# Gated linear attention on one core: decay levels grown in place on VectorE, the two head pairs' levels interleaved, the two heads' state products side by side

## Chip, cores and metric

The kernel runs on one core of a Trainium2 chip. The metric is the device time of one execution in microseconds (us); before the change it is 1471.57 us, the median of three runs (1470.83 to 1471.6). Engines are named as the profile names them: PE is TensorE's matmul, PEld its weight load, DVE is VectorE, ACT ScalarE, POOL GpSimd, SP SyncE.

## What is computed

One layer of a hybrid encoder on 512 tokens: an input projection, three token mixers side by side (windowed attention, short convolution, bidirectional gated linear attention, GLA), a merge, a LayerNorm, and an expert-choice mixture of 16 experts. The change touches GLA alone:

```python
def gla_direction(q, k, v, log_a):      # 4 heads, key dim 64, value dim 128
    b = jnp.cumsum(log_a..., axis=2)    # in chunks of C tokens
    diff = b[:, :, :, None] - b[:, :, None, :]
    decay = jnp.exp(jnp.where(lower, diff, -jnp.inf))
    scores = jnp.einsum('bnthd,bnshd,bntshd->bnhts', qc, kc, decay)
    o_intra = jnp.einsum('bnhts,bnshv->bnthv', scores, vc)
    ...
    o_inter = jnp.einsum('bnthd,bnhdv->bnthv', qc * jnp.exp(b), states)
    return (o_intra + o_inter).reshape(B, S, H, dv)
...
o = o_f + o_b                           # forward and backward scans, summed
```

A score between tokens t and s is the sum over the key dimension of q, k and the product of all decays between them. Without it the sum would be a plain product; with it the kernel has to scale q and k by decays before they meet.

## The kernel before

**Stages.** The trace has these: a first projection (to about 43 us), the main input projection with GLA and attention woven into it (to about 264 us), the merge (to about 480 us), output projection and routing (to about 530 us), and the experts, whose weights stream in through 10 tiles of 2 MB (to the end).

**The woven stage.** The main projection has 25 blocks of 128 output columns (`names`, from `gq0` to `cb3`). A block is 24 matmuls of 128x512 into one PSUM tile `pa` (L267 to L269). The work of GLA and of attention is a list of 43 steps. From the fifth block on the blocks are cut into segments (`SEGS`: eight blocks of three segments of 9, 9 and 6 matmuls, then blocks of two and of one), and one step stands behind each segment. Program order for step s is: its successor's `prep` (VectorE, GpSimd), the low half of a weight split (`wb`, VectorE, L256), the segment's matmuls, the step's own matmuls (`pe`), its evacuation (`post`). All engines work through their queues in that order.

**Levels.** The four heads come in two pairs (`Gla(0)`, `Gla(1)`; two heads of 64 lines fill 128 partitions). Scores are built level by level, for m = 1, 2, 4, ... 128: within each block of 2m tokens the tokens of one half meet those of the other, so that q carries the decay from the block's middle to it, and k the decay from it to the middle. `levels` lists 0 (the diagonal), these eight, 256 (transposed keys) and 257 (the state): 11 steps for each pair. Four decay arrays of 512 tokens are kept for a pair: `Pf` and `Sb` (used by q), `Sf` and `Pb` (used by k). At each level from m = 2, `prep` doubles the reach of all four, VectorE `Sf` and `Pf` (L376, L377), GpSimd `Pb` and `Sb` (L378, L379), and then forms decayed q (L385, L386, VectorE) and decayed k (L388, L389, GpSimd) anew into one of two tiles `qk2`; each of these eight takes half of the 512 tokens. Then 16 products of 64x64 (L421, for m below 128) go to `pg0` and `pg1`, and `post` puts them under a mask into `gD` (L446), or for m of 64 and 128 copies them into `A` (L442 to L452, ScalarE).

**Output.** `av_pe` (L463, L466) multiplies A by the values for each head and each of four token blocks tb, two products of 128x128 and then one with the state, whose weights and state fill 64 partitions only. `av_squares`, `av_var`, `av_norm`, `tr_pe` and `tr_post` follow in steps of their own.

**Order of the steps.** The 11 levels of pair 0, its `av_pe`; the 11 levels of pair 1, beside which the rest of pair 0's output runs; pair 1's `av_pe`; then attention (19 steps), beside whose first steps the rest of pair 1's output runs. [...]

Of the kernel before, what the change touches and what calls it, by code (L numbers as in the profile page):

```python
# [28 lines left out]
def tile_hybrid_layer(ctx, tc, pk, w2p, xT, x, wlv, wa, wak, wmb, wout, eg, eu, ed, out):  # L29
# [62 lines left out]
    Q = [128, 4, 512]  # L92
# [41 lines left out]
    gD = at_t[:, 384:896].rearrange("p (h b t) -> p h b t", h=2, b=4)  # L134
# [145 lines left out]
    adec = {}  # L280
# [53 lines left out]
        A.copy(h, src)  # L334
        later.append(lambda: V.tensor_sub(l, src, f32(h)))

    def qk_tiles():
        st["qk2"], st["gps1"] = D("qk2", [128, 2, 2, 512], [128, 2, 512])

    class Gla:  # L340


        def __init__(self, i):
            self.i = i
            self.q = gqk[:, 0, i, :]
            self.k = gqk[:, 1, i, :]
            self.w = {}
            self.levels = [0, 1, 2, 4, 8, 16, 32, 64, 128, 256, 257]

        def start(self):  # L350
            i = self.i
            if i == 0:
                self.ps, st["gA0"] = D("gps0", Q, Q)
                self.Pf, self.Sb, self.Sf, self.Pb = (self.ps[:, j, :] for j in range(4))
                adec[0, 0], adec[1, 0] = self.Pf, self.Sb
                adec[0, 1], adec[1, 1] = misc[:, 2, :], misc[:, 3, :]
            else:
                self.ps = st["gps1"]
                self.Pf, self.Sb = misc[:, 2, :], misc[:, 3, :]
                self.Sf, self.Pb = (self.ps[:, j, :] for j in range(2))  # L360
            G.memset(self.Sf, 1.0)
            G.memset(self.Pb, 1.0)

        def prep(self, m):

            if m == 0 and self.i == 1:
                self.start()
            if m == 0 or m == 257:
                return
            if m > 1:  # L370
                h = m // 2
                v = [a.rearrange("p (n two h) -> p n two h", two=2, h=h) for a in (self.Pf, self.Sb, self.Sf, self.Pb)]
                Pf, Sb, Sf, Pb = v
                n = 512 // m
                sh = [128, n, h]
# [4 lines left out]
            if "qk2" not in st:  # L380
                qk_tiles()
            w = st["qk2"][:, self.levels.index(m) % 2]
            self.w[m] = w
            r = lambda ap: ap.rearrange("p (n two h) -> p n two h", two=2, h=m)
            V.tensor_mul(r(w[:, 0, :])[:, :, 0, :], r(self.q)[:, :, 0, :], r(self.Sb)[:, :, 0, :])  # L385
            V.tensor_mul(r(w[:, 0, :])[:, :, 1, :], r(self.q)[:, :, 1, :], r(self.Pf)[:, :, 1, :])  # L386
            if m > 1:
                G.tensor_mul(r(w[:, 1, :])[:, :, 0, :], r(self.k)[:, :, 0, :], r(self.Sf)[:, :, 0, :])  # L388
                G.tensor_mul(r(w[:, 1, :])[:, :, 1, :], r(self.k)[:, :, 1, :], r(self.Pb)[:, :, 1, :])  # L389

        def pe(self, m):
            if m == 257:
                self.p = P("pst")
                for b in range(4):
                    for h in range(2):
                        head = 2 * self.i + h
                        PE.matmul(self.p[h * 64:h * 64 + 64, b // 2 * 128:b // 2 * 128 + 128],
                                  self.kt[:, b * 128 + h * 64:b * 128 + h * 64 + 64],
                                  v_sb[:, b, head * 128:(head + 1) * 128], start=b % 2 == 0, stop=b % 2 == 1)
                return  # L400
            w = self.w.get(m)
            q = w[:, 0, :] if m else self.q
            k = w[:, 1, :] if m > 1 else self.k
            if m == 256:
                self.p = P("pkt")
                for b in range(4):
                    PE.transpose(self.p[:, b * 128:(b + 1) * 128], k[:, b * 128:(b + 1) * 128], ident)
                return
            x = m // 128
            pp = [P("pg0"), P("pg1")]  # L410
            for b in range(4):
                for h in range(2):
                    hp = slice(h * 64, h * 64 + 64)
                    if x:
                        PE.matmul(pp[h][:, b * 128:(b + 1) * 128], k[hp, b * 128:(b + 1) * 128],
                                  q[hp, (b ^ 1) * 128:(b ^ 1) * 128 + 128], start=True, stop=True)
                        continue
                    for c in range(2):
                        s0 = b * 128 + c * 64
                        t0 = b * 128 + (c ^ (m == 64)) * 64  # L420
                        PE.matmul(pp[h][c * 64:c * 64 + 64, b * 64:b * 64 + 64], k[hp, s0:s0 + 64], q[hp, t0:t0 + 64],  # L421
                                  start=True, stop=True)
            self.p = pp

        def post(self, m):
            if m >= 256:

                t = H("gkt" if m == 256 else "gst")
                if m == 256:
                    self.kt = t  # L430
                    A.copy(t, self.p)
                else:
                    self.state = t
                    A.copy(t[:, 0:256], self.p[:, 0:256])
                return
            if m == 0:
                a = st[f"gA{self.i}"]
                self.A = [a[:, 2 * h:2 * h + 2, :] for h in range(2)]
            for h in range(2):
                p = self.p[h][:, 0:256].rearrange("p (b t) -> p b t", b=4)  # L440
                if m == 128:
                    A.copy(self.A[h][:, 1, :], self.p[h])  # L442
                elif m == 0:
                    A.activation(gD[:, h], p, AF.Copy, scale=2.0)
                elif m < 64:
                    V.copy_predicated(gD[:, h], masks[:, None, m.bit_length() - 1, :].to_broadcast([128, 4, 64]), p)  # L446
                else:
                    for c in range(2):
                        hp = slice(c * 64, c * 64 + 64)
                        d = self.A[h][hp, 0, :].rearrange("p (b t) -> p b t", b=4)  # L450
                        A.copy(d[:, :, (1 - c) * 64:(2 - c) * 64], p[hp])
                        A.copy(d[:, :, c * 64:(c + 1) * 64], gD[hp, h])  # L452

        def av_pe(self):
            self.po = [P("po0"), P("po1")]
            for h in range(2):
                head = 2 * self.i + h
                hp = slice(h * 64, h * 64 + 64)
                for tb in range(4):
                    p = self.po[h][:, tb * 128:(tb + 1) * 128]  # L460
                    for x in range(2):
                        sb = tb ^ x
                        PE.matmul(p, self.A[h][:, x, sb * 128:(sb + 1) * 128],  # L463
                                  v_sb[:, sb, head * 128:(head + 1) * 128], start=x == 0, stop=False)
                    c = (1 - tb // 2) * 128
                    PE.matmul(p, self.w[256][hp, 0, tb * 128:(tb + 1) * 128], self.state[hp, c:c + 128],  # L466
                              start=False, stop=True)

        def av_squares(self):
# [173 lines left out]
            ysplit("c", i, t)  # L643


    g0, g1 = Gla(0), Gla(1)
    g0.start()

    class Step:

# [56 lines left out]

    def main_evac(nm, p):
# [806 lines left out]
```

## Time and profile before

| | us |
|---|---|
| median of three runs | 1471.57 |
| the profiled execution, its own time | 1470.79 |
| its span, first to last instruction | 1469.0 |
| woven stage, first level product to first attention score (60.89 to 164.25) | 103.36 |
| PE busy in that stretch | 87.76 |
| DVE busy in that stretch | 74.62 |
| POOL busy in that stretch | 63.73 |

A timeline row reads: start, duration of the merged group, engine, line, operation, output and inputs, their shape, the number of instructions, and in brackets the idle time of the engine before the group and what ended it. [...] A merged group's last instruction has a tail, so that the next group can start before the row's end.

### The profile page before, as it was taken

The numbers are of one execution on the slowest core, as the hardware profiler recorded it, in microseconds if no ns is written. First come the engines' busy times: TensorE is split into PE (matmuls) and PEld (weight loads), VectorE is DVE, ScalarE is ACT, GpSimd is POOL, SyncE is SP. The second block draws the span as 40 slices with busy tenths as digits, with TensorE's granted clock in tenths as the row PEclk, the third lists the DMA queues.
The fourth block names the chain that finished last, engine by engine and source line by source line (L and its number), as shares of the span: only waits on it lengthen the run. The fifth ranks groups of instructions, "written<-read, shape, count | busy, mean of one in ns | idle before, by whom it ended". The sixth has DMA issues, their size and how long they took to land.

```text
span 1469.0 us, 17474 instructions
## 1 busy us (share of the span) xinstructions
PE 1374.3 (94%) x7458; PEld 785.2 (53%) x7458; DVE 447.0 (30%) x903; ACT 288.3 (20%) x546; POOL 87.7 (6%) x118
## 2 busy tenths in 40 slices
PE   9988999999999989999999989989989988998994
PEld 8766777888888865533533523523433433342343
DVE  5569586323345442212002002001011011101236
ACT  4523455222224121110100100100100100100011
POOL 0267200000000010000000000000000000000001
PEclk9999999999999989999999999999999999999997
DMA  6111111232237787999999999999999999999994
GB/s 227 44 59 33 54 62 69 86 103 91 95 104 303 322 328 323 427 428 428 427 427 428 428 428 428 428 427 427 427 427 429 428 428 428 428 427 427 427 381 144
DMA packets 47484, 449.28 MB, mean 306 GB/s; under 512 B 4304, under 2 KB 12624, under 8 KB 21552
## 3 DMA queue, kind: packets, MB, share of 16 engines
q1 hardware_dynamic: 47408, 448.18, 73.9%
q8 instruction: 58, 0.95, 0.3%
q14 instruction: 18, 0.15, 0.0%
HBM read 446.07 MB, written 2.10 MB: 305 GB/s over the span
## 4 chain that ended last, share of the span: by engine, by line
PE 52%; DMA 40%; DVE 6%; ACT 0%; issue 0%; POOL 0%; SPq 0%; DVEq 0%; ACTq 0%; POOLq 0%
PE pgt L1223 7%; PE pup L1223 6%; PE py L1232 4%; PE pm L874 3%; PE pm L876 3%; PE pm L875 3%; DMA e12u<-in_eu_dram 3%; DMA e8u<-in_eu_dram 3%; DMA e5g<-in_eg_dram 3%; DMA e7g<-in_eg_dram 3%; DMA e11g<-in_eg_dram 3%; DMA e15g<-in_eg_dram 3%; DMA e13g<-in_eg_dram 3%; DMA e9g<-in_eg_dram 3%; DMA e9d<-in_ed_dram 3%; DMA e6u<-in_eu_dram 3%
## 5 line engine op out<-in xcount | busy, mean ns | idle before, releaser
L1216 DVE TENSOR_TENSOR acc<-acc,pcb 128x512 f32<-128x512 f32 x64 | 41.1, 684 | 221.2 <-PE pcb L1214 221.2
L1241 DVE SCALAR_TENSOR_TENSOR yl<-py,small,late 64x512 fp32r<-64x512 f32 x30 | 22.5, 750 | 235.5 <-ACT late L1240 235.5
L1171 PEld LDWEIGHTS pxg<-Sg,xres 128*128 128x128 f32 x512 | 65.1, 196 | 50.5 <-issue 43.1
L267 PE MATMUL pa<-xh,wb 128*128 128x512 f32 x200 | 84.4, 422 | 0.0
L268 PE MATMUL pa<-xl,wb 128*128 128x512 f32 x200 | 79.6, 398 | 0.0
L269 PE MATMUL pa<-xh,wb 128*128 128x512 f32 x200 | 79.5, 397 | 0.0
L1171 PE MATMUL pxg<-Sg,xres 128*128 128x128 f32 x512 | 77.1, 294 | 0.0
L874 PE MATMUL pm<-xh,wm 128*128 128x512 f32 x192 | 74.8, 390 | 0.0
L875 PE MATMUL pm<-xl,wm 128*128 128x512 f32 x192 | 74.7, 389 | 0.0
L876 PE MATMUL pm<-xh,wm 128*128 128x512 f32 x192 | 74.7, 389 | 0.0
L1240 ACT ACTIVATE late<-py,small 64x512 fp32r<-64x512 f32 x30 | 20.5, 682 | 246.2 <-PE py L1232 234.0
L1387 ACT COPY hbt<-pht 128x512 f32<-128x512 f32 x16 | 9.4, 586 | 251.0 <-PE pht L1386 251.0
L1380 DVE TENSOR_TENSOR hbt<-pup,hbt 128x512 f32<-128x512 f32 x32 | 22.1, 691 | 111.8 <-PE pup L1223 111.8
L1397 POOL TENSOR_SCALAR small<-small 128x1 f32<-128x1 f32 x1 | 0.2, 228 | 922.8 <-DVE small L1394 922.8
L1165 DVE COPY small<-pgt 128x2 f32<-128x2 f32 x8 | 1.3, 159 | 175.7 <-PE pgt L1163 175.7
L267 PEld LDWEIGHTS pa<-xh,wb 128*128 128x128 f32 x200 | 38.3, 191 | 11.6 <-issue 2.9
L1375 ACT ACTIVATE hbt<-pgt 128x512 f32<-128x512 f32 x32 | 19.0, 597 | 126.5 <-PE pgt L1223 126.5
L227 DVE TENSOR_TENSOR wm<-wr,wm 128x1536 fp32r<-128x1536 f32 x24 | 42.0, 1751 | 4.1 <-ACT wm L224 4.1
L269 PEld LDWEIGHTS pa<-xh,wb 128*128 128x128 f32 x200 | 38.4, 192 | 8.7
L268 PEld LDWEIGHTS pa<-xl,wb 128*128 128x128 f32 x200 | 38.6, 193 | 6.7
L874 PEld LDWEIGHTS pm<-xh,wm 128*128 128x128 f32 x192 | 36.0, 188 | 7.6 <-issue 0.2
L876 PEld LDWEIGHTS pm<-xh,wm 128*128 128x128 f32 x192 | 36.0, 188 | 7.5
(420 smaller groups left out, 2410.0 us busy)
## 6 DMA issues: line engine op xcount, KB each, us to landing
wr<-in_wmb_dram SPq DMA_DIRECT2D x24, 768.0 KB, 4.2
wr<-in_wa_dram SPq DMA_DIRECT2D x12, 1024.0 KB, 4.8
e0u<-in_eu_dram SPq DMA_DIRECT2D x4, 2048.0 KB, 20.5
e0d<-in_ed_dram SPq DMA_DIRECT2D x4, 2048.0 KB, 15.2
e1g<-in_eg_dram SPq DMA_DIRECT2D x4, 2048.0 KB, 8.0
e1u<-in_eu_dram SPq DMA_DIRECT2D x4, 2048.0 KB, 12.0
e1d<-in_ed_dram SPq DMA_DIRECT2D x4, 2048.0 KB, 15.9
e2g<-in_eg_dram SPq DMA_DIRECT2D x4, 2048.0 KB, 13.3
```

Source lines behind the costliest of these rows:

```text
L227: sp2[u] = V.tensor_sub(l, raw2[u], f32(h))
L267: PE.matmul(p, w[:, 0, k, :], XH(k), start=k == 0, stop=False)
L268: PE.matmul(p, w[:, 0, k, :], XL(k), start=False, stop=False)
L269: PE.matmul(p, w[:, 1, k, :], XH(k), start=False, stop=k == 7)
L874: PE.matmul(p, h[:, k, :], XH(k), start=k == 0, stop=False)
L875: PE.matmul(p, h[:, k, :], XL(k), start=False, stop=False)
L876: PE.matmul(p, l[:, k, :], XH(k), start=False, stop=k == 7)
L1171: PE.matmul(p[:, 0:128], xr_(tb)[:, every2(d)], Sg[:, tb].rearrange("p a b -> p (a b)"), start=tb == 0, stop=tb == 3)
L1216: V.tensor_add(r, r, p)
L1223: PE.matmul(p[c][g * 64:(g + 1) * 64, :], l, w[:, g * 1024 + c * 512:g * 1024 + c * 512 + 512], start=k == 0, stop=k == 7)
L1232: PE.matmul(p[g * 64:(g + 1) * 64, :], hT[:, k % 4 * 2 + r, half * 64:(half + 1) * 64], w[:, r * 1024 + dh * 512:r * 1024 + dh * 512 + 512 ...
L1241: V.scalar_tensor_tensor(yl[pp, dh, :], p[pp, :], gate[pp, e:e + 1], f32(yh[pp, dh, :]), op0=OP.mult, op1=OP.subtract)
```

## The change

- Keys and queries are kept, decayed, in one tile `gkq` for each pair: planes 0 and 1 hold k (both are copied from PSUM), planes 2 and 3 hold q times either decay. Plane parity says whether a token lies in the first or the second half of the next block.
- At each level `prep` multiplies these planes in place: one VectorE instruction for k and one for q, each over 512 elements, which run through the half blocks of the two planes in turn (`walk`). The decay is one column for each block, read with step 0. Only the columns that the next level needs are kept of the decays, by a third, shrinking VectorE instruction. `Sf`, `Pb`, the `memset`s and all of GpSimd's level work are gone.
- For m from 2 to 32, ScalarE copies the wanted halves of k into a contiguous tile (`A.copy(self.k, ...)`); from m = 64 on k is read from its plane. q is read by the matmuls straight from the two planes, in runs of m.
- The steps of the two pairs alternate: level m of pair 0, level m of pair 1, then the next m. `gD` is kept for each pair. The output steps of both pairs come after all levels, `av_var` and later ones beside the second `av_pe` and the first attention steps.
- In `av_pe` the token block is the outer loop, and the state products of two heads stand next to each other.

```diff
         def prep(self, m):
...
-                V.tensor_mul(Sf[:, :, 0, :], Sf[:, :, 0, :], Pf[:, :, 1, h - 1:h].to_broadcast(sh))
-                V.tensor_mul(Pf[:, :, 1, :], Pf[:, :, 1, :], Pf[:, :, 0, h - 1:h].to_broadcast(sh))
-                G.tensor_mul(Pb[:, :, 1, :], Pb[:, :, 1, :], Sb[:, :, 0, 0:1].to_broadcast(sh))
-                G.tensor_mul(Sb[:, :, 0, :], Sb[:, :, 0, :], Sb[:, :, 1, 0:1].to_broadcast(sh))
...
-            V.tensor_mul(r(w[:, 0, :])[:, :, 0, :], r(self.q)[:, :, 0, :], r(self.Sb)[:, :, 0, :])
-            V.tensor_mul(r(w[:, 0, :])[:, :, 1, :], r(self.q)[:, :, 1, :], r(self.Pf)[:, :, 1, :])
-            if m > 1:
-                G.tensor_mul(r(w[:, 1, :])[:, :, 0, :], r(self.k)[:, :, 0, :], r(self.Sf)[:, :, 0, :])
-                G.tensor_mul(r(w[:, 1, :])[:, :, 1, :], r(self.k)[:, :, 1, :], r(self.Pb)[:, :, 1, :])
+            if m == 1:
+                V.tensor_mul(self.kq[:, 2:4, :], self.q[:, None, :].to_broadcast([128, 2, 512]), self.dec)
+                return
+            h = m // 2
+            n = 512 // m
+            self.k = st["qk2"][:, self.i, 0, :]
+            kq, dec = self.kq[:, 0, 0:1], self.dec[:, 0, 0:1]
+            for x, at, step in ((0, 512 + h, -512 - h), (1024, h, 512 - h)):
+                v = walk(kq, x, (m, n), (512 + h, 2), (1, h))
+                V.tensor_mul(v, v, walk(dec, at, (m, n), (step, 2), (0, h)))
+            if m < 256:
+                v = self.dec.rearrange("p a (n two h) -> p a n two h", two=2, h=h)
+                V.tensor_mul(v[:, :, :, 0, 0], v[:, :, :, 0, 0], v[:, :, :, 1, 0])
+            if m < 64:
+                A.copy(self.k, walk(kq, 0, (2 * m, n // 2), (512 + m, 2), (1, m)))
+
+        def part(self, x, hp, t0, n, m):
+
+            if m == 0 or m == 1 and x == 0:
+                return (self.q if x else self.kq[:, 0, :])[hp, t0:t0 + n]
+            if m >= n:
+                return self.kq[hp, 2 * x + t0 // m % 2, t0:t0 + n]
+            if not x:
+                return self.k[hp, t0:t0 + n]
+            return walk(self.kq[hp, 2, t0:t0 + 1], 0, (2 * m, n // (2 * m)), (512 + m, 2), (1, m))
...
         def av_pe(self):
...
-                    c = (1 - tb // 2) * 128
-                    PE.matmul(p, self.w[256][hp, 0, tb * 128:(tb + 1) * 128], self.state[hp, c:c + 128],
+                c = (1 - tb // 2) * 128
+                for h in range(2):
+                    hp = slice(h * 64, h * 64 + 64)
+                    PE.matmul(p[h], self.part(1, hp, tb * 128, 128, 256), self.state[hp, c:c + 128],
                               start=False, stop=True)
...
-    steps = level_steps(g0)
-    o0 = out_steps(g0)
-    steps.append(o0[0])
-    steps += overlay(level_steps(g1), o0[1:], 0)
-    o1 = out_steps(g1)
-    steps.append(o1[0])
-    steps += overlay([att_step(i) for i in range(len(atts) + 3)], o1[1:], 0)
+    steps = [s for both in zip(level_steps(g0), level_steps(g1)) for s in both]
+    o0, o1 = out_steps(g0), out_steps(g1)
+    o0[1].join(o1[0])
+    steps += o0[:2] + overlay(overlay([att_step(i) for i in range(len(atts) + 3)], o0[2:], 0), o1[1:], 0)
...
         elif kind == "gk":
-            A.copy(gqk[:, 1, int(nm[2]), :], p)
+            for j in range(2):
+                A.copy(st["gkq"][int(nm[2])][:, j, :], p)
```

VectorE's queue, two levels of pair 0 before the change (`gps` holds the decays, `qk` the decayed q and k, `wb` is the weight split of the projection, the last numbers are the shape):

```order
L446 COPY_PREDICATED at_t<-at_t,pg_642 128x256
L446 COPY_PREDICATED at_t<-at_t,pg_643 128x256
L376 TENSOR_TENSOR gps_395<-gps_395 128x64x4
L377 TENSOR_TENSOR gps_395<-gps_395 128x64x4
L385 TENSOR_TENSOR qk_558<-v_sb,gps_395 128x32x8
L386 TENSOR_TENSOR qk_558<-v_sb,gps_395 128x32x8
L446 COPY_PREDICATED at_t<-at_t,pg_683 128x256
L446 COPY_PREDICATED at_t<-at_t,pg_684 128x256
L376 TENSOR_TENSOR gps_395<-gps_395 128x32x8
L377 TENSOR_TENSOR gps_395<-gps_395 128x32x8
```

The same queue after the change, a level of pair 0 (decays in `v_sb`) and of pair 1 (decays in `at_t`):

```order
L438 COPY_PREDICATED at_t<-at_t,pg_764 128x256
L438 COPY_PREDICATED at_t<-at_t,pg_765 128x256
L368 TENSOR_TENSOR gkq<-gkq,v_sb 128x64x2x4 x2
L371 TENSOR_TENSOR v_sb<-v_sb 128x128
L255 TENSOR_TENSOR wb_378<-wr,wb_378 128x1024
L438 COPY_PREDICATED at_t<-at_t,pg_799 128x256
L438 COPY_PREDICATED at_t<-at_t,pg_800 128x256
L368 TENSOR_TENSOR gkq<-gkq,at_t 128x64x2x4 x2
L371 TENSOR_TENSOR at_t<-at_t 128x128
```

Four instructions of 256 elements between two masked copies have become two of 512 and one short one, and the level that follows belongs to the other pair.

GpSimd's queue before the change, two levels of pair 0:

```order
L378 TENSOR_TENSOR gps_395<-gps_395 128x64x4
L379 TENSOR_TENSOR gps_395<-gps_395 128x64x4
L388 TENSOR_TENSOR qk_558<-v_sb,gps_395 128x32x8
L389 TENSOR_TENSOR qk_558<-v_sb,gps_395 128x32x8
L378 TENSOR_TENSOR gps_395<-gps_395 128x32x8
```

GpSimd's queue after the change, from the constants to the routing:

```order
L136 IOTA iab 128x128
L137 IOTA iab 128x128
L529 TENSOR_SCALAR qk_396<-at_t 128x384 x8
L923 MEMSET one 128x1
L924 MEMSET one 128x2
```

All 68 instructions of the levels are gone from GpSimd (95 rows of its queue have become 27); what is left there is the attention bias (L529).

TensorE's queue at the start of `av_pe` of pair 1, before the change (`po0`, `po1` are the two heads, `gst` the state; in brackets what an instruction waits for):

```order
L463 MATMUL po0_1387<-v_sb_102,rsil_660 128x128 [waits PE_49]
L463 MATMUL po0_1387<-v_sb_102,rsil_660 128x128
L466 MATMUL po0_1387<-gst_1379,qk2_558 128x128 [waits DVE_49,Activation_49]
L463 MATMUL po0_1387<-v_sb_102,rsil_660 128x128 x2
L466 MATMUL po0_1387<-gst_1379,qk2_558 128x128
```

And after it:

```order
L454 MATMUL po0_1278<-v_sb_102,rsil_644 128x128 [waits PE_49]
L454 MATMUL po0_1278<-v_sb_102,rsil_644 128x128
L454 MATMUL po1_1279<-v_sb_102,rsil_644 128x128 [waits PE_49]
L454 MATMUL po1_1279<-v_sb_102,rsil_644 128x128
L459 MATMUL po0_1278<-gst_1222,gkq_395 128x128 [waits DVE_49,Activation_49]
L459 MATMUL po1_1279<-gst_1222,gkq_395 128x128
L454 MATMUL po0_1278<-v_sb_102,rsil_644 128x128 x2
```

TensorE now goes from 128 partitions to 64 and back four times for a pair instead of eight times. The number of its instructions is the same.

## Rows read from the trace of the kernel before

**Rows 1.** The page's 40 slices of the span: busy tenths.
```profile
PE   9988999999999989999999989989989988998994
...
POOL 0267200000000010000000000000000000000001
```

**Rows 2.** Stretches of the woven stage: PE, PEld, DVE, ACT, POOL busy; PEclk; DMA.
```profile
60.89:101.20 40.31, 32.30 (x384) 23.88 (x383) 34.26 (x50) 14.88 (x27) 31.00 (x35) 0.96 0.18 66
...
109.30:152.90 43.60, 36.00 (x396) 26.88 (x396) 39.51 (x69) 13.52 (x31) 30.39 (x33) 0.92 0.14 49
...
60.89:164.25 103.36, 87.76 (x884) 65.65 (x883) 74.62 (x120) 34.42 (x85) 63.73 (x70) 0.95 0.13 47
...
138.00:140.00 2.00, 2.00 (x6) 1.52 (x6) 2.00 (x4) 0.00 (x0) 1.92 (x3) 0.50 0.00 0
```

**Rows 3.** Waits of PE from 60.89 to 164.25: total us, times, longest.
```profile
PE pg L421 <- DVE qk L386: 12.0, 8, 2.9
PE pg L415 <- DVE qk L386: 1.4, 2, 0.8
PE pt L493 <- DVE gon L485: 1.2, 1, 1.2
PE pkt L407 <- POOL qk L389: 0.9, 2, 0.4
```

**Rows 4.** Timeline of one level of pair 0, VectorE, GpSimd and PE.
```profile
82.92 0.90 POOL L389 TENSOR_TENSOR qk<-v_sb,gps 128x256 f32<-128x256 f32 x1
83.16 0.94 DVE L386 TENSOR_TENSOR qk<-v_sb,gps 128x256 f32<-128x256 f32 x1
...
84.02 0.77 DVE L446 COPY_PREDICATED at_t<-at_t,pg 128x256 f32<-128x256 int32 x2
...
84.25 0.69 PE L421 MATMUL pg<-qk 64*64 64x64 f32 x32 [1.81 <-DVE qk L386]
```

**Rows 5.** Timeline of PE: three level products that waited for nothing.
```profile
111.30 0.69 PE L421 MATMUL pg<-v_sb 64*64 64x64 f32 x32
114.19 0.69 PE L421 MATMUL pg<-qk,v_sb 64*64 64x64 f32 x32
116.41 0.69 PE L421 MATMUL pg<-qk 64*64 64x64 f32 x32
```

**Rows 6.** Single prices: timeline rows, and a line's min/median/max in ns.
```profile
57.49 1.28 DVE L318 TENSOR_TENSOR zmn<-zmn,pz 128x512 f32<-128x512 f32 x2
109.14 0.43 DVE L385 TENSOR_TENSOR qk<-v_sb,at_t 128x256 f32<-128x256 f32 x1 [12.04 <-PE po L466]
122.70 0.62 ACT L334 CAST yg<-gy 128x512 fp32r<-128x512 f32 x1 [5.60 <-DVE gy L500]
L256 DVE TENSOR_TENSOR wb<-wr,wb x25: 1207/1219/1870, 23.3 to 252.0; 128x1024 fp32r<-128x1024 f32 x25
```

**Rows 7.** VectorE's groups by line: busy and mean ns of one; elements read apart, and adjacent.
```profile
L1056 DVE TENSOR_REDUCE Sg<-Sg 128x16 f32<-128x128 f32 x2 | 0.6, 360 | 0.0
L1154 DVE TENSOR_TENSOR Sg<-pk,iota 128x128 f32<-128x128 f32 x64 | 14.3, 285 | 0.5
```

**Rows 8.** Timeline of PE: output products of pair 0, and a level product on 64 partitions.
```profile
91.59 1.16 PE L415 MATMUL pg<-qk 64*128 64x128 f32 x16 [0.63 <-DVE qk L386]
...
102.69 0.71 PE L463 MATMUL po<-v_sb,gps 128*128 128x128 f32 x4
103.33 0.48 PE L466 MATMUL po<-gst,qk 64*128 64x128 f32 x2
103.75 0.71 PE L463 MATMUL po<-v_sb,gps 128*128 128x128 f32 x4
```

**Rows 9.** Timeline of VectorE: its one longer pause in attention's first steps.
```profile
175.44 0.56 DVE L564 CUSTOM_DVE_ANT_0 ap<-ps,qk 128x384 f32<-128x384 f32 x1 [1.74 <-PE ps L553]
```

**Rows 10.** Stretches after routing began, columns as in group 2.
```profile
500.00:520.00 20.00, 18.94 (x116) 16.49 (x114) 15.24 (x62) 3.17 (x9) 0.79 (x5) 0.98 0.50 195
...
700.00:800.00 100.00, 99.77 (x508) 41.95 (x504) 13.33 (x23) 10.11 (x18) 0.00 (x0) 1.00 1.01 427
```

More of the change, by code (lines that the diff above doesn't have):

```diff
@@ L133, in tile_hybrid_layer @@
     masks = at_t[:, 0:384].bitcast(I32).rearrange("p (a b) -> p a b", a=6)
-    gD = at_t[:, 384:896].rearrange("p (h b t) -> p h b t", h=2, b=4)
     iab = H("iab", I32)
@@ L335, in ysplit, with walk @@
         later.append(lambda: V.tensor_sub(l, src, f32(h)))
-    def qk_tiles():
-        st["qk2"], st["gps1"] = D("qk2", [128, 2, 2, 512], [128, 2, 512])
+    def walk(base, at, *dims):
+        return bass.AP(tensor=base.tensor, offset=base.offset + at, ap=[base.ap[0]] + [list(d) for d in dims])
     class Gla:
@@ L345, in __init__ @@
             self.q = gqk[:, 0, i, :]
-            self.k = gqk[:, 1, i, :]
-            self.w = {}
+            self.dec = gqk[:, 1] if i == 0 else misc[:, 2:4, :]
+            for d in range(2):
+                adec[d, i] = self.dec[:, 1 - d, :]
+            self.gD = at_t[:, 384 + 512 * i:896 + 512 * i].rearrange("p (h b t) -> p h b t", h=2, b=4)
             self.levels = [0, 1, 2, 4, 8, 16, 32, 64, 128, 256, 257]
[L350 to L362, printed above, removed]
+            self.kq = st["gkq"][i]
@@ L364, in prep @@
         def prep(self, m):
-            if m == 0 and self.i == 1:
-                self.start()
             if m == 0 or m == 257:
                 return
-            if m > 1:
[L371 to L375, printed above, removed]
-                V.tensor_mul(Sf[:, :, 0, :], Sf[:, :, 0, :], Pf[:, :, 1, h - 1:h].to_broadcast(sh))
-                V.tensor_mul(Pf[:, :, 1, :], Pf[:, :, 1, :], Pf[:, :, 0, h - 1:h].to_broadcast(sh))
-                G.tensor_mul(Pb[:, :, 1, :], Pb[:, :, 1, :], Sb[:, :, 0, 0:1].to_broadcast(sh))
-                G.tensor_mul(Sb[:, :, 0, :], Sb[:, :, 0, :], Sb[:, :, 1, 0:1].to_broadcast(sh))
@@ L380, in prep @@
[L380 to L384, printed above, removed]
-            V.tensor_mul(r(w[:, 0, :])[:, :, 0, :], r(self.q)[:, :, 0, :], r(self.Sb)[:, :, 0, :])
-            V.tensor_mul(r(w[:, 0, :])[:, :, 1, :], r(self.q)[:, :, 1, :], r(self.Pf)[:, :, 1, :])
-            if m > 1:
-                G.tensor_mul(r(w[:, 1, :])[:, :, 0, :], r(self.k)[:, :, 0, :], r(self.Sf)[:, :, 0, :])
-                G.tensor_mul(r(w[:, 1, :])[:, :, 1, :], r(self.k)[:, :, 1, :], r(self.Pb)[:, :, 1, :])
+            if m == 1:
+                V.tensor_mul(self.kq[:, 2:4, :], self.q[:, None, :].to_broadcast([128, 2, 512]), self.dec)
+                return
@@ L400, in pe @@
                 return
-            w = self.w.get(m)
-            q = w[:, 0, :] if m else self.q
-            k = w[:, 1, :] if m > 1 else self.k
             if m == 256:
@@ L406, in pe @@
                 for b in range(4):
-                    PE.transpose(self.p[:, b * 128:(b + 1) * 128], k[:, b * 128:(b + 1) * 128], ident)
+                    PE.transpose(self.p[:, b * 128:(b + 1) * 128], self.part(0, slice(0, 128), b * 128, 128, m), ident)
                 return
@@ L414, in pe @@
                     if x:
-                        PE.matmul(pp[h][:, b * 128:(b + 1) * 128], k[hp, b * 128:(b + 1) * 128],
-                                  q[hp, (b ^ 1) * 128:(b ^ 1) * 128 + 128], start=True, stop=True)
+                        PE.matmul(pp[h][:, b * 128:(b + 1) * 128], self.part(0, hp, b * 128, 128, m),
+                                  self.part(1, hp, (b ^ 1) * 128, 128, m), start=True, stop=True)
                         continue
@@ L420, in pe @@
                         t0 = b * 128 + (c ^ (m == 64)) * 64
-                        PE.matmul(pp[h][c * 64:c * 64 + 64, b * 64:b * 64 + 64], k[hp, s0:s0 + 64], q[hp, t0:t0 + 64],
-                                  start=True, stop=True)
+                        PE.matmul(pp[h][c * 64:c * 64 + 64, b * 64:b * 64 + 64], self.part(0, hp, s0, 64, m),
+                                  self.part(1, hp, t0, 64, m), start=True, stop=True)
             self.p = pp
@@ L435, in post @@
                 return
-            if m == 0:
+            if m == 64:
                 a = st[f"gA{self.i}"]
                 self.A = [a[:, 2 * h:2 * h + 2, :] for h in range(2)]
+            gD = self.gD
             for h in range(2):
@@ L455, in av_pe @@
             self.po = [P("po0"), P("po1")]
[L456 to L460, printed above, removed]
+            for tb in range(4):
+                p = [self.po[h][:, tb * 128:(tb + 1) * 128] for h in range(2)]
+                for h in range(2):
+                    head = 2 * self.i + h
                     for x in range(2):
                         sb = tb ^ x
-                        PE.matmul(p, self.A[h][:, x, sb * 128:(sb + 1) * 128],
+                        PE.matmul(p[h], self.A[h][:, x, sb * 128:(sb + 1) * 128],
                                   v_sb[:, sb, head * 128:(head + 1) * 128], start=x == 0, stop=False)
-                    c = (1 - tb // 2) * 128
-                    PE.matmul(p, self.w[256][hp, 0, tb * 128:(tb + 1) * 128], self.state[hp, c:c + 128],
+                c = (1 - tb // 2) * 128
+                for h in range(2):
+                    hp = slice(h * 64, h * 64 + 64)
+                    PE.matmul(p[h], self.part(1, hp, tb * 128, 128, 256), self.state[hp, c:c + 128],
                               start=False, stop=True)
@@ L643, in conv_evac @@
             ysplit("c", i, t)
+    st["gkq"] = D("gkq", Q, Q)
     g0, g1 = Gla(0), Gla(1)
-    g0.start()
+    st["qk2"], st["gA0"] = D("qk2", [128, 2, 2, 512], Q)
     class Step:
```

## Prediction

> **What bounds the kernel now.** I read the page's slices first. PE is busy nearly throughout, and POOL works only in slices 2 to 5, the one part of the span in which PE falls to 8 tenths before the merge [rows 1]. The stretches then give that part: of the 103.36 us from the first level product to the first attention score PE is busy 87.76, so 15.6 are lost, and they lie in the two stretches of levels, in which VectorE is busy 85% and 91% of the time and GpSimd 77% and 70% [rows 2]. PE's own waits there add up to the same: 12.0 + 1.4 + 1.2 + 0.9 = 15.5, nearly all before level products and put down to the decayed q of VectorE [rows 3]. One level shows why: L386 takes 0.94 beside GpSimd's L389 of 0.90, and the product starts 0.15 after L386 ends, having waited 1.81 [rows 4]. L385, its twin, took 0.43 when GpSimd was idle [rows 6]. So VectorE and GpSimd slow each other here, and the chain decays, q and k, product, masked copy is what ends last. [...]
>
> **What goes.** (1) The waits: 15.5. (2) The clock: 40.31 x 0.04 + 43.60 x 0.08 = 1.6 + 3.5 = 5.1 us of full-speed time are not granted. Part of that lies in waits already counted, so I take 4.5; the bounds are 0, if other pauses keep the clock low, and 5.1. Together that is 20.0 us if nothing is late in the place of GpSimd and the old chain.
>
> **What is late next: VectorE.** Steps of PE that waited for nothing follow each other after 2.89 us with nine projection matmuls and 2.22 with six [rows 5]; a block of three steps is 8.00, a step 2.67 on the average. A step of VectorE after the change has the two masked copies (0.77 [rows 4]), two products of 512 elements, a shrinking one on the decays, and a third of a weight split (1.22 / 3 = 0.41 [rows 6]). For 512 elements the rows give 0.64 (two in 1.28), and half of the 1.22 for 1024 is 0.61 [rows 6]; I take 0.64. The shrinking ones cost about 0.64, 0.43 [rows 6], 0.28 [rows 7] and then, as an estimate, 0.2. So the steps need 0.77 + 1.28 + 0.41 = 2.46 and 0.64, 0.43, 0.28, 0.2: 3.10 for m = 2, 2.89 for 4, 2.74 for 8, 2.66 for 16, 32 and 64. Two pairs make 2 x 16.71 = 33.4 for twelve steps, against PE's 12 x 2.67 = 32.0: VectorE falls behind by 1.4. It may: from the end of one product of a pair to the start of its next PE has two steps less the product itself, 5.34 - 0.69 = 4.65, and the chain through VectorE is 0.77 + 0.64 + 0.64 = 2.05, so 2.6 us of lag cost nothing. I charge 1.0 for uneven steps. The wait that the change adds is that of the products in place: level 2m of a pair can't be formed before level m has been read. It is queued behind the masked copies, which wait for the same product anyway, and what stands behind it (the weight split, the other pair's level) is needed a step or more later.
>
> ScalarE's copies of k (ten) and the second copies of k out of PSUM (two) are 0.62 each [rows 6]. ScalarE is busy 34.42 of 103.36 [rows 2], and the copy runs beside the q product of VectorE; I cost it at nothing. Without that cover it would put 0.62 on a chain that has 2.6 to spare.
>
> The elements of a walk lie apart in memory, which no multiply of the trace before shows in that form. The nearest rows are a reduction that reads 16 elements apart, 360 ns for 128 elements, and a multiply of adjacent ones, 285 ns [rows 7]: 0.59 ns more for each element, 0.30 for 512, so 0.94 in place of 0.64. From below nothing is to be gained against 0.61. I take 0.64, since L385 took 0.43 for its 256 elements although it reads and writes half blocks with gaps [rows 6]. [...]
>
> **State products.** A run of two passes on 64 partitions holds PE from 103.33 to 103.75, 0.42 us, while sixteen passes of that kind in one run, the heads alternating, take 1.16, or 0.07 each [rows 8]. So a run of two has about 0.27 of turning. Eight such runs in a pair become four: 4 x 0.27 = 1.1 us, 2.2 for both pairs. If the way back to 128 partitions costs as much, it is 4.4. I take 3.2; 0 is the lower bound, should the turning belong to the instruction and not to the change of partitions.
>
> **Output steps beside attention.** Pair 0's norm, gating and splitting (six instructions of 512 elements and ten short ones, about 4 + 2 us of VectorE) move from the levels to the first attention steps. There VectorE paused 1.74 us [rows 9], and PE's own step is longer by pair 0's transposes, about 1.2 us that it no longer spends among the levels. What is left over, some 1 to 2 us, delays single softmax steps; I charge 0.7 (bounds 0 and 4.0 - 1.74 = 2.3).
>
> **Does it reach the end?** The weights of the experts stream at a DMA share of 1.01 from 700 to 800 us, but of 0.50 from 500 to 520 [rows 10]: the stream had stood still for want of free tiles, and goes on when PE frees them. So whatever PE gains before routing moves the restart, and with it the end, one for one.
>
> **Sum.** 15.5 + 4.5 + 3.2 - 1.0 - 0.7 = 21.5 us. The profiled execution took 1470.79 us, its span 1469.0 and 1.79 around it; 1470.79 - 21.5 = 1449.3. The median of the runs is 0.78 above the profiled execution, so I predict 1450.
>
> **Rivals.**
> - A: VectorE becomes the bound, because its walks cost 0.94. Each of the twelve steps then needs 0.60 more, 7.2 in all; with 1.4 of lag and a slack of 2.6 - 0.6 the levels wait 6.6, 5.6 more than charged: about 1456. For it: VectorE's need and PE's are within 5% of each other already. Against it: L385's 0.43. [...]
> - B: PE reads the walked q more slowly. At the same 0.59 ns for an element, 64 columns and 16 products cost 0.6 in a step, twelve steps 7.2: about 1457. No row of before shows PE reading in that way.
> - C, slower: products in place leave VectorE at most one step ahead of PE, so that a dear walk is paid in full. Beyond 0.64 each extra e costs 2e in each of some seventeen steps, 34e, less about 3.4 of room in the light steps. That eats the 22.5 us that the change saves without waits when e = 0.76, at a price of 1.40, 2.2 times the contiguous one; at 1.55 the time is about 1475. Against it: nothing in the rows makes a multiply more than 1.5 times dearer by its steps.
> - D, no change: the stream of weights, not PE, sets the end from routing on, and the time stays 1471. Against it speaks the idle half of the DMA engines from 500 to 520.
>
> **How the numbers follow.** Forecast 0.73, A 0.13, B 0.07, C 0.04, D 0.03. The least time is that with 4.4 for the state products, 5.1 for the clock and no charge: 25.0 us, 1446.6 against the median; allowing for a clock that falls elsewhere, 1445. The upper end takes in A and B: 1458. A measurement can tell about 0.2% from no change, 3 us. Faster: the forecast, A and B, 0.93; same 0.03; slower 0.04.
>
> **What would show it.** Right: from the first level product to the first score about 80 us (103.36 less 22.2 and the transposes); POOL there busy some 2 us, only with the bias; the clock 1.00 in both halves; PE's waits before level products under 2 us in all; L368 near 0.65 to 0.7 us; state runs of four passes under 0.6 us; and the restart of the weights earlier by the same 21 us as the end. Wrong: L368 above 0.9 us with PE waiting on it (A), level products well above 0.69 us (B), waits of PE among attention's first steps, or a router stage whose clock is lower than before.

## Result and profile after

The changed kernel takes 1446.62 us (median of four runs, 1446.25 to 1447.54), the kernel before beside it 1471.59. The ratio is 0.9834, with a 95% interval of 0.9822 to 0.9846: 25.0 us less, where 1450, 21.5 less, was forecast. The profiled span went from 1469.0 to 1444.5.

The page's slices of the changed kernel, as [rows 1]: PE no longer falls in slices 3 and 4, and POOL is nearly idle in slices 2 to 5.

```profile
PE   9999999999999899999999989979979989998994
...
POOL 0010100000000100000000000000000000000002
```

Stretches, columns as in [rows 2], where PEclk is the clock granted to TensorE as a share of its full one, and the last two numbers are the busy share of the DMA engines and GB/s: all from the first level product to the first attention score, then the first half of the levels, then the rest of them with the transposed keys and the state.

```profile
60.95:138.00 77.05, 76.75 (x878) 58.92 (x877) 50.72 (x94) 38.67 (x93) 5.55 (x4) 1.00 0.18 63
60.95:85.90 24.95, 24.64 (x365) 18.26 (x368) 22.22 (x35) 13.09 (x22) 0.00 (x0) 1.00 0.23 73
85.90:120.00 34.10, 34.10 (x394) 25.96 (x395) 26.21 (x49) 20.02 (x38) 5.55 (x4) 1.00 0.24 88
```

The stage is 77.05 us long in place of 103.36; TensorE is idle for 0.30 us of it in place of 15.6, and its clock is 1.00 throughout. All of its waits there and in the attention behind it (to 264 us), as [rows 3]:

```profile
PE pg L412 <- ACT qk L373: 0.3, 1, 0.3
...
PE pp L582 <- DVE ap L576: 0.4, 1, 0.4
```

TensorE's timeline shows level products that wait for nothing, and the one that waits; those of m = 1 last 0.89 us, the others 0.69 to 0.73:

```profile
66.06 0.89 PE L412 MATMUL pg<-gkq 64*64 64x64 f32 x32
...
72.25 0.73 PE L412 MATMUL pg<-gkq,qk 64*64 64x64 f32 x32
...
85.81 0.69 PE L412 MATMUL pg<-gkq,qk 64*64 64x64 f32 x32 [0.30 <-ACT qk L373]
```

VectorE's timeline, level m = 2 of pair 0 and then m = 4 of it:

```profile
67.73 2.19 DVE L368 TENSOR_TENSOR gkq<-gkq,v_sb 128x512 f32<-128x512 f32 x2
69.95 0.69 DVE L371 TENSOR_TENSOR v_sb<-v_sb 128x512 f32<-128x512 f32 x1
...
75.84 1.28 DVE L368 TENSOR_TENSOR gkq<-gkq,v_sb 128x512 f32<-128x512 f32 x2
77.15 0.66 DVE L371 TENSOR_TENSOR v_sb<-v_sb 128x256 f32<-128x256 f32 x1
```

The two products in place take 1.28 us from m = 4 on, and 2.19 for m = 2 alone. Output products of pair 1, as [rows 8], from their start to the projection matmul behind them: a run of four state passes holds TensorE from 130.05 to 130.47, 0.42 us, which is what a run of two held it before.

```profile
129.07 1.05 PE L454 MATMUL po<-v_sb,rsil 128*128 128x128 f32 x8
130.05 0.49 PE L459 MATMUL po<-gst,gkq 64*128 64x128 f32 x4
130.47 1.16 PE L454 MATMUL po<-v_sb,rsil 128*128 128x128 f32 x8
...
135.00 0.50 PE L266 MATMUL pa<-xh,wb 128*128 128x512 f32 x1
```

The same products of pair 1 in the kernel before, their start and the matmul behind them:

```profile
152.97 0.60 PE L463 MATMUL po<-v_sb,rsil 128*128 128x128 f32 x4
...
161.31 0.50 PE L267 MATMUL pa<-xh,wb 128*128 128x512 f32 x1
```

**Where the 25 us lie.** The stage is 26.3 shorter. Waits went from 15.5 to 0.3, 15.2. The output products of a pair take 5.93 (129.07 to 135.00) where they took 8.34 (152.97 to 161.31), 2.41, for both pairs 4.8: of the 2.41, 1.7 lie in the state runs (8 x 0.42 became 4 x 0.42) and 0.7 in the passes between them. Pair 0's transposes, 0.84 (142.22 to 143.06), now stand behind the first score and are no gain. The products of m = 1 and 2 cost 0.5 more. What is left of the 26.3 is 5.9, of which the clock explains some 5.1 (its share not granted in the windows of before); 0.8 stays unassigned. Attention gives back the 0.84 and a wait of 0.4, so 25.1 should leave it. Routing's products of `pbc` begin at 499.12 in place of 523.66, 24.5 earlier; the 0.6 between is not assigned. From there it reaches the end: the span is 24.5 shorter. The lines, before and after:

```profile
523.66 6.52 PE L1117 MATMUL pbc<-Sg,one 128*128 128x128 f32 x32 [1.95 <-POOL Sg L1113]
```
```profile
499.12 6.75 PE L1109 MATMUL pbc<-Sg,one 128*128 128x128 f32 x32 [1.95 <-POOL Sg L1105]
```

### The profile page after: what moved, and what is told of

Its sections match the earlier page's. It is cut to its first block, busy times and chain, and to the rows that moved or that the text cites. A ratio compares the mean times of both kernels' runs of the same rounds, so it can differ in the third digit from the quotient of the medians.

```text
span 1444.5 us, 17364 instructions
## 1 busy us (share of the span) xinstructions
PE 1364.9 (94%) x7458; PEld 779.4 (54%) x7458; DVE 427.1 (30%) x883; ACT 295.0 (20%) x558; POOL 28.6 (2%) x50
## 4 chain that ended last, share of the span: by engine, by line
PE 55%; DMA 41%; DVE 3%; issue 0%; ACT 0%; SPq 0%; POOL 0%; DVEq 0%; ACTq 0%
PE pgt L1215 7%; PE pup L1215 6%; PE py L1224 4%; PE pa L266 3%; PE pm L866 3%; PE pm L867 3%; PE pm L868 3%; DMA e8u<-in_eu_dram 3%; DMA e12u<-in_eu_dram 3%; DMA e5g<-in_eg_dram 3%; PE pa L268 3%; PE pa L267 3%; DMA e13g<-in_eg_dram 3%; DMA e9g<-in_eg_dram 3%; DMA e11d<-in_ed_dram 3%; DMA e6u<-in_eu_dram 3%
## 5 line engine op out<-in xcount | busy, mean ns | idle before, releaser
L867 PEld LDWEIGHTS pm<-xl,wm 128*128 128x128 f32 x192 | 36.0, 188 | 7.5
```

Source lines behind the costliest of these rows:

```text
L867: PE.matmul(p, h[:, k, :], XL(k), start=False, stop=False)
```

## Experiments

**Does VectorE have room left?** One more multiplication for each pair and level:

```diff
+            pad = st["qk2"][:, self.i, 1, :]
+            if m == 2:
+                G.memset(pad, 1.0)
+            V.tensor_mul(pad, pad, pad)
             h = m // 2
```

> The changed kernel with one more multiplication of 512 elements on VectorE for each pair and level from m = 2, ahead of the level's products, on a tile that nothing reads: sixteen times 0.66 us. It measures the room that VectorE has left. The prediction's sum (case A): 0.6 more in each of twelve steps costs 5.6 us over the charge of 1.0, so some 6.6 on waits that are now 0.3: 1452 to 1454. Theory from the changed kernel's trace (VectorE runs without a pause from 65 to 105 us and TensorE just begins to wait): nearly all of 12 x 0.66 is paid, 6.5 to 8 us: 1454. Rival (two steps of slack are still there): under 1 us, 1447.

It takes 1453.49 (ratio 0.988, 0.9865 to 0.9894), 6.9 more than the changed kernel (its profiled span is 6.1 longer), as both the prediction's price and the changed kernel's trace had it. TensorE's waits of the stage, and the added line:

```profile
PE pg L416 <- ACT qk L377: 4.8, 6, 1.3
PE pg L416 <- DVE gkq L372: 1.3, 2, 1.0
...
L365 DVE TENSOR_TENSOR qk<-qk 128x512 f32<-128x512 f32 x16 | 11.0, 686 | 0.0
```

Of 16 x 0.69 = 11.0 us of work 5.8 became waits before level products (6.1 against 0.3). The changed kernel stands at the edge: VectorE is filled in its levels (busy 39.50 of the 40.00 us from 65 to 105), and TensorE waits only 0.3.

**Interleaving alone, and in place without interleaving.** The changed kernel with the pairs in turn:

```diff
+        def post(m, nxt):
+            g.post(m)
+            if nxt > 1:
+                g.prep(nxt)
...
-    steps = [s for both in zip(level_steps(g0), level_steps(g1)) for s in both]
+    steps = level_steps(g0) + level_steps(g1)
```

> The changed kernel without the interleaving: all levels of pair 0, then all of pair 1, each level's products in place formed behind the masked copies of the level before (they can't be formed earlier). GpSimd stays free. Theory (interleaving is needed for the chain): from the end of a product to the start of the next of its pair TensorE has a segment of 1.5 to 2.1 us, the chain of masked copies 0.77, k 0.64 and its copy 0.62 needs 2.05 and more, for the smallest levels 0.9 more, so that each of some sixteen steps waits 0.3 to 0.9: 8 us, with 1 to 2 of clock, 1455 (1451 to 1461). Rival (it is GpSimd's leaving alone that took the waits away): under 2 us of waits, 1447 to 1449.

It takes 1453.44 (0.988, 0.9865 to 0.9895), 6.9 more. Its stage, its waits there, and the longest of them:

```profile
60.57:144.50 83.93, 77.01 (x876) 58.95 (x875) 51.28 (x94) 38.48 (x93) 5.74 (x4) 1.00 0.16 58
...
PE pg L412 <- ACT qk L373: 3.5, 3, 1.4
PE pg L412 <- DVE gkq L368: 2.6, 2, 1.8
PE pg L412 <- DVE gkq L360: 0.6, 1, 0.6
PE pg L406 <- DVE gkq L368: 0.3, 1, 0.3
...
68.36 0.73 PE L412 MATMUL pg<-gkq,qk 64*64 64x64 f32 x32 [1.76 <-DVE gkq L368]
```

The total fits the expectation, its spread does not: not every step waits a little, seven of them wait, for the first levels and where a weight split lies ahead of the masked copies. The clock stays at 1.00 with 7.0 us of waits in all.

The other half, the kernel before with the levels interleaved (and the output steps behind all levels, as in the changed kernel):

```diff
-            w = st["qk2"][:, self.levels.index(m) % 2]
+            w = st["qk2"][:, self.i]
...
-    steps = level_steps(g0)
...
+    steps = [s for both in zip(level_steps(g0), level_steps(g1)) for s in both]
```

> The kernel before with only the interleaving: the levels of the two pairs alternate, the output steps stand as in the changed kernel, each pair has its own masked tile and one tile of decayed q and k; decays and products are still split between VectorE and GpSimd. Theory (the two engines slow each other, so that VectorE's throughput is the limit): a level needs 0.63 + 0.52 + 0.91 + 0.97 for its four products, 0.87 for the copies and 0.53 for a third of a split, 4.4 us, against 2.67 for a step of TensorE; the waits go from the chain to VectorE and at most a third of the 15.5 is won: 1463 to 1471, most likely 1467. Rival (interleaving alone took the waits away): waits under 3 us and the clock at 1.00, 1452 to 1454.

It takes 1467.18 against 1471.29 (0.9972, 0.9962 to 0.9982). Its levels up to m = 64, its waits, and its q products:

```profile
61.21:119.78 58.57, 46.77 (x643) 34.54 (x642) 55.80 (x88) 19.31 (x36) 49.25 (x54) 0.94 0.18 64
...
PE pg L419 <- DVE qk L384: 11.7, 9, 2.0
...
L384 DVE TENSOR_TENSOR qk<-v_sb,gps 128x256 f32<-128x256 f32 x9 | 8.8, 974 | 0.0
```

VectorE is busy 55.80 of 58.57 us: with the chain relieved it is the throughput of VectorE beside GpSimd that TensorE waits for, 0.97 us for a product that alone takes 0.43 [rows 6]. The four corners (the last is the changed kernel beside the runs on the state products below, where the kernel before took 1470.69):

| | pairs in turn | interleaved |
|---|---|---|
| levels split with GpSimd | 1471.29 | 1467.18 |
| in place on VectorE, new output order | 1453.44 | 1446.59 |

The output order is worth 4.4 (below). So the products in place, with GpSimd out, are worth 13.4 in turn and 16.2 interleaved; interleaving is worth 4.1 with the split work and 6.9 in place. How much of the 13.4 and 16.2 is the contention with GpSimd and how much the smaller number of products, these runs don't divide; the next ones bear on the contention alone.

**GpSimd beside VectorE.** Products on GpSimd that nothing reads:

```diff
+            pad = st["qk2"][:, self.i, 1, :]
+            if m == 2:
+                G.memset(pad, 1.0)
+            for e in (0, 256, 0, 256):
+                G.tensor_mul(pad[:, e:e + 256], pad[:, e:e + 256], pad[:, e:e + 256])
```

> The changed kernel with GpSimd given work in the levels again: for each pair and level from m = 2 four multiplications of 256 elements on a tile that nothing reads, as many and as long as before the change (about 0.7 to 0.9 us each). Nothing waits for them but themselves. Theory (VectorE's products stretch beside GpSimd's, 0.43 to 0.95 for 256 elements): the 32 products of 512 elements, 0.68 us now, take 1.0 to 1.4 beside GpSimd, VectorE falls behind by 10 us or more, and TensorE waits for it: 1455 to 1465, most likely 1459. Rival (GpSimd beside VectorE costs nothing, the chain was the cause): 1446.6 to 1447.6, products at 0.68.

The time, 1461.69 (0.9935, 0.9919 to 0.9952), is as expected, but for another reason. Since nothing held them, the products ran from 32 to 72 us, ahead of all levels, and of the 15.1 lost 13.0 are one wait there, behind which TensorE is slower for a while: its projection matmuls stand 0.43 us apart from 73.6 to 75.7, and 0.23 from 77.4 on (the clock is 0.74 from 54 to 73, 0.98 from 73 to 153); the levels themselves run without further waits (0.3, as in the changed kernel):

```profile
PE pa L268 <- DVE wb L255: 13.0, 1, 13.0
...
54.51 18.42 DVE L255 TENSOR_TENSOR wb<-wr,wb 128x1024 fp32r<-128x1024 f32 x1 [5.17 <-ACT wb L251]
...
35.54 36.31 POOL L366 TENSOR_TENSOR qk<-qk 128x256 f32<-128x256 f32 x60
```

So this run says nothing on the levels. A second one ties the products to them, by reading the copy of k:

```diff
                 A.copy(self.k, walk(kq, 0, (2 * m, n // 2), (512 + m, 2), (1, m)))
+                pad = st["qk2"][:, self.i, 1, :]
+                for e in (0, 256):
+                    G.tensor_mul(pad[:, e:e + 256], self.k[:, e:e + 256], self.k[:, e:e + 256])
```

> The changed kernel with two multiplications of 256 elements on GpSimd for each pair and level from m = 2 to 32, which read the fresh copy of k and write a tile that nothing reads: twenty in all, and because they read that copy they can't run ahead of their level, as those of the run before did. They begin when VectorE has the second product, the short one on the decays, the next masked copies and the other pair's products in its queue. Theory (products of two inputs on VectorE take about twice their time beside GpSimd, 0.43 to 0.95 in the kernel before, masked copies do not): each adds 0.25 to 0.5 us to VectorE, which has nothing to spare in the first twelve steps: 5 to 10 us, 1451 to 1457, most likely 1454, with products of 512 elements well above 0.68 in some levels. Stronger form (a product of VectorE stands still while GpSimd has products to do): 20 x 0.61 = 12 us, 1459. Rival (no contention in the levels): 1446.6 to 1447, products at 0.68.

It takes 1450.12 (0.9859, 0.9841 to 0.9876), 3.5 more than the changed kernel, less than the 5 expected at least. VectorE and GpSimd in one of these levels and the next, and VectorE in a later one:

```profile
69.80 0.98 DVE L371 TENSOR_TENSOR v_sb<-v_sb 128x512 f32<-128x512 f32 x1
70.70 0.77 DVE L441 COPY_PREDICATED at_t<-at_t,pg 128x256 f32<-128x256 int32 x2
...
74.44 1.63 DVE L255 TENSOR_TENSOR wb<-wr,wb 128x1024 fp32r<-128x1024 f32 x1
...
82.06 1.64 DVE L368 TENSOR_TENSOR gkq<-gkq,v_sb 128x512 f32<-128x512 f32 x2
...
69.61 1.64 POOL L376 TENSOR_TENSOR qk<-qk 128x256 f32<-128x256 f32 x2 [67.29 <-ACT qk L373]
73.35 1.63 POOL L376 TENSOR_TENSOR qk<-qk 128x256 f32<-128x256 f32 x2 [2.11 <-ACT qk L373]
```

Contention is real: L371 takes 0.98 in place of 0.69, the split 1.63 in place of 1.22 and the two products of a later level 1.64 in place of 1.28, while the masked copies keep their 0.77. TensorE waits 3.6 in the stage in place of 0.3, nearly all of the loss. The engines' busy times over the whole span, the changed kernel's and this run's:

```profile
PE 1364.9 (94%) x7458; PEld 779.4 (54%) x7458; DVE 427.1 (30%) x883; ACT 295.0 (20%) x558; POOL 28.6 (2%) x50
```
```profile
PE 1363.7 (94%) x7458; PEld 777.6 (54%) x7458; DVE 431.0 (30%) x883; ACT 294.7 (20%) x558; POOL 44.6 (3%) x70
```

VectorE's busy time rises by 3.9 us (431.0 against 427.1) for 16.0 us more of GpSimd (44.6 against 28.6), 0.24 us for each us of it. By that rate GpSimd's 63.73 us [rows 2] would have cost the kernel before some 15 us of VectorE (an estimate). The strong form is refuted: only part of GpSimd's time is added.

Why did one split last 18.42? The run that ran ahead, with six products for four:

> The run in which GpSimd's multiplications ran ahead of the levels, with six of them for each pair and level in place of four: 96 in a row instead of 64. In that run they ran from 32 to 72 us, ahead of all levels, and one weight split on VectorE that began at 54.5 us, 1.22 us long elsewhere, ended only at 72.9, when GpSimd's row of products was over; two splits before it, also beside GpSimd, took 1.31 and 1.23. If VectorE stands still until GpSimd's row ends, the row now ends 32 x 0.57 = 18 us later, near 90 us, the split lasts some 36 us, and the time is 1461.7 + 18 = 1480. If it is held for a fixed time or by something else, the time stays near 1462.

A single run takes 1476.86, beside 1472.12 for the kernel before. An earlier split, the one that is held, and GpSimd's row:

```profile
38.12 1.31 DVE L255 TENSOR_TENSOR wb<-wr,wb 128x1024 fp32r<-128x1024 f32 x1 [1.35 <-ACT wb L251]
...
54.42 33.90 DVE L255 TENSOR_TENSOR wb<-wr,wb 128x1024 fp32r<-128x1024 f32 x1 [5.17 <-ACT wb L251]
...
36.60 54.48 POOL L366 TENSOR_TENSOR qk<-qk 128x256 f32<-128x256 f32 x90
```

The standstill grew by 15.5 us with a row that is 18.2 longer. It is not a fixed time, then, and it follows the row. It doesn't end with it exactly: here at 88.3, some 3 us ahead of the row's end, in the run before 1.1 behind it, by a profile whose times on GpSimd are rough. Why two splits of the same kind at 38 and 44 us, also beside that row, took 1.31 and 1.23 stays open.

**State products.** The changed kernel with the old order of output products (heads outside, token blocks inside):

> The changed kernel with the output products in the old order (heads outside, token blocks inside), so that eight runs of two state passes stand for each pair instead of four of four. The prediction priced the new order at 3.2 us, between 0 and 4.4. The two traces say more: the output products of one pair take 8.34 us in the kernel before and 5.93 in the changed one, 2.41 for a pair, 4.8 for both. Theory by the traces: 1451.4. By the prediction's term: 1449.8. By its lower bound: 1446.6.

> The changed kernel as it is, beside the other two on the same chip, so that differences of one to five microseconds can be read against it: 1446.6, ratio 0.983.

It takes 1450.98 (0.9865, 0.9851 to 0.9878), the changed kernel beside it 1446.59 (0.9834, 0.9821 to 0.9848): 4.4, above the forecast's 3.2 and near the 4.8 of the rows. To see why, the state products of two token blocks were joined:

```diff
...
+            for tb in (0, 2):
+                values(tb, True)
+                states(tb, False)
+                states(tb + 1, True)
+                values(tb + 1, False)
```

> The changed kernel, with the state products of two token blocks next to each other (the sum of the odd blocks begins with the state product), so that a run of state products on 64 partitions has eight passes and there are two of them for a pair instead of four. Theory of the prediction, that a run pays a fixed turning of 0.27 us and 0.07 per pass: four turnings fewer and four ways back fewer in all, some 2.2 us less than 1446.6, near 1444.5. Theory from the changed kernel's trace, where a run of four passes holds the engine 0.42 us as the run of two did before, so that the two heads' products run side by side: a run of eight takes about 0.42 + 0.29 = 0.71 us against 2 x 0.42, and about 0.09 less at the way back; some 0.2 us at each of four joins, 0.9 us in all: 1445.7. Rival, that each pair of products costs 0.42 wherever it stands: no change, 1446.6.

It takes 1444.89 (0.9825, 0.9811 to 0.9838). TensorE's timeline, pair 1:

```profile
128.72 1.05 PE L455 MATMUL po<-v_sb,rsil 128*128 128x128 f32 x8
129.70 0.71 PE L463 MATMUL po<-gst,gkq 64*128 64x128 f32 x8
130.35 2.05 PE L455 MATMUL po<-v_sb,rsil 128*128 128x128 f32 x16
132.33 0.71 PE L463 MATMUL po<-gst,gkq 64*128 64x128 f32 x8
...
133.89 0.48 PE L266 MATMUL pa<-xh,wb 128*128 128x512 f32 x1
```

A run of eight passes takes 0.65 (129.70 to 130.35). Two passes of one head 0.42, four of two heads 0.42, eight of two heads 0.65: a turning of 0.27 with 0.07 for each pass would give 0.41, 0.55, 0.83. The rows fit another sum (an estimate from them): a turning of 0.19 for a run and 0.115 for each pass of one head, while the other head's passes, which use the other half of the partitions, run beside them. For the sixteen alternating passes of [rows 8] it gives 1.11, where 1.16 with its tail was measured. The way back costs about as much as the turning: between state runs eight passes of values take 1.09 (130.47 to 131.56 in the changed kernel) and sixteen 1.98 (130.35 to 132.33 here), so eight more take 0.89, and 0.20 is left for each stretch of values between two runs. That the second head's passes are hidden is inferred; no run has four passes of one head alone. The pair's output takes 5.17 (128.72 to 133.89) against 5.93, 1.5 less for both, the runs 1.7 less; the intervals overlap, so that the rows, not the times, carry this. It is the fastest kernel here.

**Products that read single elements.** The q of m = 1 from one plane:

```diff
-            if m >= n:
+            if m >= n or m == 1:
```

> The changed kernel with the q of level m = 1 read from one plane, adjacent elements, instead of single elements from two planes in turn; this level's scores are then wrong and the rest is unchanged. The products of m = 1 took 0.89 us where all others took 0.69 to 0.73. If reading single elements from two planes is the cause (case B of the prediction, in its smallest level alone), they fall to 0.69 and the stage is 0.4 us shorter; if it is something else at this place of the program (the first products of the new tile, their weights), they stay at 0.89.

```profile
65.99 0.69 PE L412 MATMUL pg<-gkq 64*64 64x64 f32 x32
```

They fall from 0.89 to 0.69: reading single elements from two planes in turn costs TensorE 0.2 us in a level product; runs of two cost 0.04 (0.73), longer ones nothing (0.69). The stage is not 0.4 us shorter, as expected: from the first level product to the first attention score it takes 76.96 (60.88 to 137.84) where the changed kernel's timeline has 77.00 (60.95 to 137.95). The first product of m = 2 comes 0.4 earlier; 0.13 of that goes into the wait at m = 8, 0.43 in place of 0.30, the rest in small pieces that no wait of the profile explains. The time, 1447.19 in a single run, can't tell 0.4 us.

## Why the prediction was right, step by step

- **Waits, 15.5: right.** 15.2 went. That the two engines slow each other and that the chain ends last are both shown, but the prediction didn't divide them: interleaving alone brought 4.1, since VectorE beside GpSimd was at its limit then (busy 55.80 of 58.57 us).
- **Clock, 4.5 (0 to 5.1): at its upper end.** It is 1.00 in the whole stage, for 0.96 and 0.92 in the levels before and 0.50 from 138 to 140 us, behind the longest wait, 2.9 [rows 2, rows 3]. Not every wait was followed by a lower one: seven of up to 1.8, 7.0 in all, left it at 1.00 (pairs in turn). With 12.1 of them (before, interleaved) the levels have 0.94; there projection matmuls kept their 0.23 us from start to start behind the longest, 2.0 up to 79.5 us, and stood 0.43 apart from 92.7 to 95.2, as they do at 0.50 in the kernel before (138.2 to 139.9), after waits of 1.3 and 1.9 between 85.3 and 91.5. Whether one of them lowers it, and which, stays open.
- **VectorE's lag, 1.0: near in size, mis-built, and so in part luck.** The rows give 0.3 of waits. Two prices were low: the products of m = 2 (1.09 for 0.64) and the short ones on the decays (256 elements 0.66 for 0.43). With these a pair needs 18.2 in place of 16.7, 36.3 for both against TensorE's 32.0, a lag of 4.3, more than the 2.6 allowed. It hardly showed because VectorE had a start: the products in place of m = 2 of pair 0 were done at 69.9, and TensorE came to them at 72.25, 2.3 later. For the next five steps VectorE took 15.7 (to 85.65), TensorE without its wait 13.3, and there, at m = 8 of pair 1, stands the wait of 0.30. It is put down to ScalarE's copy of k, which the forecast cost at nothing: there it ends at 85.75, 0.1 behind VectorE. The run with added work shows that nothing more was left; case A was close, and its price (5.6 over the charge) right.
- **Walks.** The forecast's 0.64 held from m = 4 on, and at m = 2 even the bound of 0.94 was passed, with 1.09, 0.9 ns more for an element. There, neighbouring elements lie in two planes. The decays' short product of m = 4 paid as much: its elements are 16 bytes apart, and 256 of them take 0.66 where L385 took 0.43, again 0.9 ns for each.
- **State products, 3.2 (0 to 4.4): the term that was mis-sized,** with 4.4 by the runs and 4.8 by the rows. Its mechanism was right as far as it went: by the sum above, eight turnings and eight ways back fewer are 16 x 0.19 = 3.0 of the 4.8 (an estimate). What it lacked, by the same sum, is that one head's passes run beside the other's, some 1.8 more. Its 0.07 for a pass came from a run in which the heads alternate [rows 8], so that by this sum its turning of 0.27 was too large.
- **Case B: true in kind, not in size.** 0.2 in two products, nothing from m = 4 on.
- **Attention's first steps, 0.7:** a wait of 0.4, beside the 0.84 of transposes that the sum left out on both sides, and 0.6 before routing that is not assigned. GpSimd's bias took 5.55 us, not 2, and lay beside level products at 94.6 (L368 there 1.59 for two), hidden.
- **One for one to the end: right.** Routing 24.5 earlier, the span 24.5. So case D falls. Case C needed a price of 1.40 at all levels; it was 0.64.

The forecast is 3.5 us too little by the medians and 3.0 by the profiled spans: the state products (1.2 to 1.6), the clock (0.6 to 1.4), the lag (0.7) and attention's first steps (0.3), less the 0.5 of the walked q, are 2.3 to 3.5, and the 0.6 not assigned goes off that.

## What to carry to other kernels

Where two engines share a chain and both look busy, price the work with one of them gone: a product of 0.43 us that takes 0.95 beside the other engine is not relieved by a better order (0.97 with the levels interleaved). Interleaving two independent chains took waits away here, and paid in full only once the engines had throughput to spare (6.9 us, against 4.1 while VectorE was filled beside GpSimd). Put products that fill half of the partitions next to those that fill the other half (4.4 us here).

## What the runs showed of the hardware

- A row of GpSimd products without pauses held a VectorE product of two inputs for 18.42 and 33.90 us instead of 1.22. The first of these is as long as some thirty of the GpSimd products (18.42 / 0.61). Two splits beside the same row that took 1.31 and 1.23 show that it does not always come.
- GpSimd products in pairs, tied to the levels, stretched VectorE's products of two inputs from SBUF: 0.98 us for 0.69, 1.63 for 1.22, 1.64 for 1.28 (two). The masked copies, one of whose inputs is in PSUM, took 0.77 beside GpSimd as without it. Whether the place of the inputs is the cause was not shown.
- VectorE paid 0.9 ns more for each element in the products whose neighbours lie in two planes (m = 2: 1.09 us for 0.64) or 16 bytes apart (256 elements: 0.66 for 0.43); TensorE paid 0.2 us in 0.69 for reading single elements from two planes.
- State products of two heads, on different halves of the partitions, held TensorE no longer than those of one: 0.42 us for four passes as for two, 0.65 for eight.
